# A two-layer hybrid decoder on one Trainium2 core: first stage with scaled evacuations on VectorE, layout copies partly on GpSimd, projections ahead of matrices, and an output projection that sums attention first

## The chip, the core and the metric

The kernel runs on one core of one Trainium2 chip. The core has a matrix engine (TensorE, PE in the profile, with its weight loads shown apart as PEld), VectorE (DVE), ScalarE (ACT), GpSimd (POOL) and a queue that issues most of the transfers (SyncE, SP). The engines run side by side, each through its own queue in order, and wait for each other on semaphores. SBUF is the working memory with 128 partitions; PSUM holds the results of matmuls in banks of 512 float32 columns.

The metric is the device time of one execution in microseconds. Three executions of the kernel before took 1601.77, 1602.78 and 1603.46 us, so the median is 1602.78 us.

## The reference, cut to what is computed

Batch 1, 256 tokens, width 1024, two layers. The change touches layer 0's mixing stage and, by a shared function, the output projections.

```python
h = rmsnorm(x, norm_mix[0]); memn = rmsnorm(mem, norm_mem[0])
p = h @ w_in_a[0]                        # 1024 columns: 768 for S5, 256 for the queries
mix = s5_mixer(p[..., :768], ...)        # 48 groups x 16 channels, 64 complex states each
ca = memory_cross_attn(p[..., 768:], memn, w_kv_mem[0])      # 4 heads of 64
x = x + concat([mix, ca], -1) @ w_out[0]
x = x + swiglu(rmsnorm(x, norm_ffn[0]), ffn_w_gate[0], ffn_w_up[0], ffn_w_down[0])
# layer 1: RWKV-7 mixing | cross-attention with norm_mem[1], w_kv_mem[1]; then top-2-of-8 experts
return rmsnorm(x, norm_final)

def s5_mixer(u, ...):                    # per group: state x_t = a * x_{t-1} + B_bar u_t  (complex, diagonal a)
    y = Re(C x) + d_skip * u             # B_bar and a are worked out from lam, log_dt, b
    y = gelu(y); return y * sigmoid(y @ w_glu + b_glu)
```

## The kernel before, in words

The program is one long function, `build`, without loops on the device. A planner orders it: it walks the traced instructions with a time model and gives each engine the ready instruction that stands earliest in the program. What stands earlier in the source therefore has priority, but each engine's queue is fixed before the run, and it is worked off in order. A block `with tc.issue_after(ins)` pins what is traced in it behind `ins` on its engine.

Everything that the change touches lies in the first stage (from the pools named `psA`, `wpA`, `acA`, `wkA`, `s5`) and in `outproj`, which opens the second stage. The first stage does, in program order:

- **Normalised input.** `rstd` and a scaled copy give `xh`; `transT` (L193) transposes four 128x128 blocks to one PSUM tile and evacuates them, each times its gain column, into `hT`: blocks 0 and 2 on ACT (L207), blocks 1 and 3 on DVE (L205). Four such calls fill `hT` (8 blocks x 256 tokens).
- **Parameters.** Many small DVE operations on 128x24 tiles turn lambda, dt and B, C into `wre, wim` (for B) and `are, aim` (powers of a).
- **Matrices B.** `blocks` (L488) multiplies `bnat` with `wre, wim` on DVE (two L494 and one L495 a call) and copies the result to `BN` on ACT (two L498 a call). It is called for 12 of the 24 state blocks at a time. Then `cT` and `C0` are copied out of a transposed C on ACT (L515); `cT` takes over the buffer `n1` of `bnat`.
- **Projections.** `project(n)` (L522) multiplies `hT` with 256 columns of `w_in_a` (L529) for n = 0..3: 0 to 2 are the S5 inputs, 3 the queries. It copies the PSUM tile to `U` in a token order by four (L534) and then, with 16 copies of 32 partitions out of PSUM (L538, ACT), to `Um`, the layout that the state matmuls read. The projection's weights are two halves of 512 KB in a ring of four buffers (`wpA`).
- **Local matrices.** With `BN` and `C0`, 384 passes of 32x32 blocks (L577) make `KD_`, which ACT copies out (L581); 48 transposes of `BN` (L585) make `BT`, copied by ACT (L586). `project(2)` is pinned behind the last of these transposes (L589).
- **Memory.** The generator `memory` (L540) normalises and transposes the two halves of `mem`, and evacuates each block twice, times the gains of layer 0 and of layer 1, into `memT[0]` and `memT[1]` (L556, ACT, 32 of them).
- **Rotation.** `Ec, Es` (cosine and sine per time step) are doubled up on DVE (L605 to L610), then `blocks` is called again for `CA` (which is the same memory as `BN`).
- **The loop over q = 0..5.** `front(q)`: 16 passes (L671) from `BT` and `Um`, the rotation (L675 to L678) and two scans (L681) on DVE. `back(q)`: two products on POOL (L688, L689), sums on DVE, matmuls with `KD_` (L695) and `CA` (L701), gelu (L707), the gate matmul (L710), tanh (L711) and the pair `cat0` in high and low part (L713 to L715). Three steps of a `filler` stand between front and back: `keys_values(0)` (L644, 64 passes), `cross` for two token halves, and `keys_values(1)`; what is left of it comes after the loop.
- **Output projection.** `outproj` (L280) loads `w_out` in two tiles of 2 MB; `split` cuts each into four parts of two k-blocks, a high part by a cast on ACT (L183) and a low part by a subtraction on DVE (L184), and `mm3` multiplies three products per k (L189 to L191). The k-blocks 0 to 5 of `cat0` are the S5 part, 6 and 7 the attention. The buffer of the first `w_out` tile (`wpB`) lies on the four buffers of `wpA`, whose last readers are the matmuls of `keys_values(1)`.

Layer 0's feed-forward, the RWKV stage and the experts follow, and are not touched except that layer 1 calls the same `transT` and `outproj`.

Of the kernel before, what the change touches and what calls it, by code (L numbers as in the profile page):

```python
# [9 lines left out]
F32 = mybir.dt.float32  # L10
# [3 lines left out]
OP = mybir.AluOpType  # L14
# [3 lines left out]
P = 128  # L18
# [31 lines left out]
def build(ctx, tc, a, out, taps=None):  # L50
# [57 lines left out]
    def col(nm, i):  # L108
        j = COL[nm] + i
        return cols[:, j:j + 1]  # L110

    def colb(nm, n, w):
        return cols[:, COL[nm]:COL[nm] + n, None].to_broadcast([P, n, w])

    def wload(k, n, *parts, size=2048, cut=1):

        t = ring["w"].tile([P, size], F32, name="w", tag="w")
        v = t[:, :k * n].rearrange("p (k n) -> p k n", n=n)
        for c0, ap in parts:
            src = ap.rearrange("(k p) n -> p k n", p=P)  # L120
            for i in range(0, k, k // cut):
                with ExitStack() as s_:
                    if isinstance(ring["w"], Ring) and "last" in ring:
                        s_.enter_context(tc.issue_after(ring["last"].ins))
                    ring["last"] = dma(v[:, i:i + k // cut, c0:c0 + ap.shape[1]], src[:, i:i + k // cut])
        return v
# [39 lines left out]
        return (pl.tile(shape, F32R, name=name + "h", tag=name + "h", **kw),  # L166
                pl.tile(shape, F32R, name=name + "l", tag=name + "l", **kw))

    def split(pl, w, parts, size=4096, eng=None, last=None):

        k, n = w.shape[1], w.shape[2]
        kp = k // parts if k % parts == 0 else -(-k // parts)
        for k0 in range(0, k, kp):
            kn = min(kp, k - k0)
            src = w[:, k0:k0 + kn, :]
            hi, lo = mkpair(pl, [P, size // parts], "ws")
            hv, lv = (t[:, :kn * n].rearrange("p (k n) -> p k n", n=n) for t in (hi, lo))
            if last and k0:
                with tc.issue_after(last[0]), tc.issue_after(last[1]):
                    S.copy(hv, src)  # L180
                    G.tensor_sub(lv, src, hv.bitcast(F32))
            else:
                S.copy(hv, src)  # L183
                (eng or V).tensor_sub(lv, src, hv.bitcast(F32))  # L184
            yield hv, lv, k0
# [7 lines left out]
    def transT(src, h, q, tr, gain, f32=None, pair=None, act=False):  # L193

        hs = slice(h * P, (h + 1) * P)
        t = tr()
        for j in range(4):
            k = 4 * q + j
            r = TE.transpose(t[:, j, :], src[:, k * P:(k + 1) * P], ident).ins
        for j in range(4):  # L200
            k = 4 * q + j
            g = col(gain[0], gain[1] + k)
            if f32 is not None:
                if j % 2 and not act:
                    V.tensor_scalar(f32[:, k, hs], t[:, j, :], g, None, op0=OP.mult)  # L205
                else:
                    S.activation(f32[:, k, hs], t[:, j, :], AF.Copy, scale=g)  # L207
            if pair:
                S.activation(pair[0][:, k, hs], t[:, j, :], AF.Copy, scale=g)
                V.scalar_tensor_tensor(pair[1][:, k, hs], t[:, j, :], g, pair[0][:, k, hs].bitcast(F32),  # L210
                                       op0=OP.mult, op1=OP.subtract)
        return r
# [67 lines left out]
    def outproj(i, cp, ws, mm, order):  # L280


        for n in range(2):
            ns = slice(n * 512, (n + 1) * 512)
            w = wload(KD, 512, (0, a["w_out"][i][:, ns]), size=4096)
            ps = [mm() for _ in range(NH)]

            def part(h, wh, wl, k0):
                hs = slice(h * P, (h + 1) * P)
                for j in range(2):  # L290
                    k = k0 + j
                    mm3(ps[h], (cp[0][:, k, hs], cp[1][:, k, hs]), wh[:, j, :], wl[:, j, :], k == 0, k == KD - 1)
            ps_ = []
            for p_ in split(ws, w, 4):
                part(0, *p_)
                ps_.append(p_)
            resid(0, n, ps[0])
            yield 0, n
            for j_, p_ in enumerate(ps_):
                with ExitStack() as s_:  # L300
                    if n and j_ > 1 and j_ - 4 >= -len(order):
                        s_.enter_context(tc.issue_after(order[j_ - 4]))
                    part(1, *p_)
            resid(1, n, ps[1])
            yield 1, n


    with ExitStack() as st:
# [188 lines left out]
                s = slice(64 * g, 64 * g + 64)  # L497
                S.copy(v[s, :, :, g, :], m1[s])  # L498

        b0, b1 = bnat[:, 0], bnat[:, 1]  # L500
        for i0 in (0, 12):
            blocks(BN, 0, (b0, b1), wre, wim, OP.subtract, i0, 12)
            blocks(BN, 1, (b1, b0), wre, wim, OP.add, i0, 12)
        cT = su.tile([P, 2, NST, 16], F32, name="cT", tag="n1")
        for ri, sg in ((0, 1.0), (1, -1.0)):
            t = tr()
            for b in range(3):
                TE.transpose(t[:, b, :], cnat[:, ri, 2 * b:2 * b + 2].rearrange("c q p -> c (q p)"), ident)
            tv = t[:, 0:3, :].rearrange("s b (i g j) -> s b i g j", i=4, g=2)
            for d, js in ((cT[:, ri], None), (C0[:, :, ri], True)):  # L510
                dv = d.rearrange("s (b r i) j -> s b r i j", b=3, r=2)
                for r in range(2):
                    for g in range(2):
                        o = dv[64 * g:64 * g + 64, :, r]
                        S.activation(o[:, :, :, 16 * g:16 * g + 16] if js else o, tv[64 * r:64 * r + 64, :, :, g, :],  # L515
                                     AF.Copy, scale=sg)

        U = sp.tile([P, QC, 4, NC], F32, name="U")
        Um = sp.tile([P, NST, NC], F32, name="Um")
# [2 lines left out]
        def project(n):  # L522
            w = w0 if n == 0 else halves(a["w_in_a"][0][:, n * T:(n + 1) * T])
            ps = mm().rearrange("p (c t) -> p c t", c=2)
            for t_ in ((slice(0, P), slice(P, T)) if n == 0 else (slice(0, T),)):
                for c in range(2):
                    cs = slice(c * P, (c + 1) * P)
                    for k in range(KD):
                        TE.matmul(ps[:, c, t_], w[k // 4][:, k % 4, cs], hT[:, k, t_], start=k + c + t_.start == 0,  # L529
                                  stop=k == KD - 1, skip_group_check=True)  # L530
            if n == 3:
                S.copy(qT, ps)
                return
            S.copy(U[:, 2 * n:2 * n + 2], ps.rearrange("p c (t s) -> p c s t", s=4))  # L534
            for w_ in range(4):
                for m in range(4):
                    src = ps[32 * w_:32 * w_ + 32].rearrange("p c (t s) -> p c t s", s=4)[:, :, :, 3 - m]
                    S.copy(Um[32 * m:32 * m + 32, 8 * n + w_:8 * n + 8:4], src)  # L538

        def memory():  # L540

            for h in range(NH):
                m = wk.tile([P, D], F32, name="mrow", tag="xh", bufs=2)
                dma(m, mem[h * P:(h + 1) * P, :])
                xh = wk.tile([P, D], F32, name="xh", tag="xh", bufs=2)
                rs = rstd(m, xh)
                S.activation(xh, m, AF.Copy, scale=rs)
                for q in range(2):
                    t = tr()
                    for j in range(4):  # L550
                        k = 4 * q + j
                        TE.transpose(t[:, j, :], xh[:, k * P:(k + 1) * P], ident)
                    for i in range(2):
                        for j in range(4):
                            k = 4 * q + j
                            S.activation(memT[i][:, k, h * P:(h + 1) * P], t[:, j, :], AF.Copy,  # L556
                                         scale=col("nmem", i * KD + k))
                yield

        memT = [ac.tile([P, KD, T], F32, name="memT", tag=f"memT{i}", bufs=1) for i in range(2)]  # L560
        mem_ = memory()
        project(0)
        project(1)

        id32 = su.tile([P, 32], F32, name="id32")
        V.tensor_reduce(id32, ident.rearrange("p (w c) -> p c w", w=4), axis=AX.X, op=OP.add)
# [2 lines left out]
        for q0, n in ((0, 4), (4, 2)):  # L569
# [9 lines left out]
            for w_ in range(4):  # L579
                o = slice(32 * w_, 32 * w_ + 32)  # L580
                S.copy(KD_[o, q0:q0 + n, :, o], tv[o, :n])  # L581
        for i in range(0, NST, 2):
            t = tr()
            for j in range(4):
                bt_ = TE.transpose(t[:, j, :], BN[:, i + j // 2, j % 2, :], ident).ins  # L585
            S.copy(BT[:, i:i + 2].rearrange("p i r s -> p (i r s)"), t.rearrange("p j s -> p (j s)"))  # L586

        next(mem_)
        with tc.issue_after(bt_):  # L589
            project(2)  # L590
        next(mem_)
        project(3)

# [18 lines left out]
                cn, sn = double(4 * n, cn, sn)  # L612
            n *= 2

        for i0 in (0, 12):
            blocks(CA, 0, (cT[:, 0], cT[:, 1]), are, aim, OP.add, i0, 12)
            blocks(CA, 1, (cT[:, 1], cT[:, 0]), are, aim, OP.subtract, i0, 12)

        with tc.issue_after(early[0]):
            G.memset(gmask, 1.0)  # L620
# [1172 lines left out]
```

## Time and profile before

| what | us |
|---|---|
| median of three executions | 1602.78 |
| the profiled execution's own time | 1604.18 |
| its span, first to last instruction | 1602.4 |
| S5 part of the first stage ends (last `cat0` pair) | 151.5 |
| first matmul of the output projection | 155.8 |

The page of the profile shows all engines over the span: PE busy 95%, DVE 80%, ACT 68%, POOL 9%. These shares belong to the experts above all, which take the larger part of the span. The first stage, about a tenth of the span, has to be read by itself: with the view of stretches, which gives each engine's busy time between two moments, and with the timeline, which lists the instructions in order of time (start, duration, engine, line, operation, output and inputs, count, and in brackets the idle time before with what ended it).

### The profile page before, as it was taken

The page shows a single profiled execution, that of the slowest core. Times are in us where ns is not written, and L with a number is a line of the kernel's source. Part 1 is how long each engine was busy: PE and PEld are TensorE (multiplying, and loading weights), DVE is VectorE, ACT ScalarE, POOL GpSimd, SP SyncE. Part 2 cuts the span into 40 slices and gives each one's busy share as a digit, 9 for nine tenths or more (in the row PEclk, how much of TensorE's full clock was granted, in tenths as well). Part 3 has the DMA queues.
Part 4 walks back from the last instruction along what each step waited for, and adds up shares of the span by engine and source line. Part 5 has one row for each costly group of instructions (what it writes and reads, how often), then busy time and mean ns, then how long its engine had stood idle before and what let it go on. Part 6 is the DMA issues. An engine that isn't in the chain of part 4 may idle for free. (4 is left out here: it accounts for less than half of the span.)

```text
span 1602.4 us, 21869 instructions
## 1 busy us (share of the span) xinstructions
PE 1515.7 (95%) x8465; PEld 1272.6 (79%) x8465; DVE 1276.7 (80%) x1567; ACT 1087.6 (68%) x1417; POOL 139.9 (9%) x183
## 2 busy tenths in 40 slices
PE   5798999998969889999999999999999999999996
PEld 4686888887968768888888888888888888888885
DVE  7744655545796568899899899899899898988986
ACT  6765554435634337777787787787777778777774
POOL 2033000003564130000000000000000000000000
PEclk9799999999989989999999999999999999999999
DMA  6023654622310677999999999999999999999970
GB/s 181 15 93 127 238 199 143 217 99 89 122 50 21 224 285 275 347 374 356 342 379 354 345 374 360 343 370 366 339 369 367 363 349 362 350 356 365 355 278 29
DMA packets 198031, 423.46 MB, mean 264 GB/s; under 512 B 13952, under 2 KB 35614, under 8 KB 197918
## 3 DMA queue, kind: packets, MB, share of 16 engines
q1 hardware_dynamic: 195746, 419.29, 71.5%
q10 hardware_dynamic: 2172, 2.68, 0.5%
q8 instruction: 68, 1.11, 0.3%
q14 instruction: 45, 0.37, 0.1%
HBM read 420.91 MB, written 1.05 MB: 263 GB/s over the span
## 5 line engine op out<-in xcount | busy, mean ns | idle before, releaser
L184 DVE TENSOR_TENSOR wsl<-w,wsh 128x1024 fp32r<-128x1024 f32 (+1 forms) x757 | 894.2, 1216 | 149.9 <-ACT wsh L183 138.1
L183 ACT CAST wsh<-w 128x1024 fp32r<-128x1024 f32 (+1 forms) x757 | 783.4, 1049 | 248.9 <-PE gu L191 95.6
L190 PE MATMUL gu<-wsl,xeh 128*128 128x512 f32 x896 | 350.0, 391 | 0.0
L189 PE MATMUL gu<-wsh,xeh 128*128 128x512 f32 x896 | 348.1, 395 | 1.6 <-DVE xs L1697 1.6
L191 PE MATMUL gu<-wsh,xel 128*128 128x512 f32 x896 | 348.9, 389 | 0.0
L189 PEld LDWEIGHTS gu<-wsh,xeh 128*128 128x128 f32 x896 | 168.3, 188 | 37.3 <-ACT wsh L183 2.4
L191 PEld LDWEIGHTS gu<-wsh,xel 128*128 128x128 f32 x896 | 168.2, 188 | 35.3 <-DVE xel L1472 0.4
L190 PEld LDWEIGHTS gu<-wsl,xeh 128*128 128x128 f32 x896 | 168.2, 188 | 34.8
L190 PE MATMUL yac<-wsl,ath 128*128 128x512 f32 x440 | 173.0, 393 | 0.0
L191 PE MATMUL yac<-wsh,atl 128*128 128x512 f32 x440 | 171.7, 390 | 0.0
L189 PE MATMUL yac<-wsh,ath 128*128 128x512 f32 x440 | 136.3, 391 | 0.0
L277 POOL TENSOR_TENSOR rs<-vv,mhalf 128x1 f32<-128x1 f32 x8 | 4.4, 557 | 1204.8 <-DVE vv L276 1204.8
L191 PEld LDWEIGHTS yac<-wsh,atl 128*128 128x128 f32 x440 | 82.7, 188 | 17.1
L189 PEld LDWEIGHTS yac<-wsh,ath 128*128 128x128 f32 x440 | 82.2, 188 | 16.9
L190 PEld LDWEIGHTS yac<-wsl,ath 128*128 128x128 f32 x440 | 82.8, 188 | 15.4
L190 PE MATMUL mm<-wsl,hTh 128*128 128x512 f32 (+1 forms) x192 | 71.3, 371 | 0.0
L189 PE MATMUL mm<-wsh,hTh 128*128 128x512 f32 (+1 forms) x192 | 71.1, 374 | 0.0
L191 PE MATMUL mm<-wsh,hTl 128*128 128x512 f32 (+1 forms) x192 | 70.3, 372 | 0.0
L1659 ACT CAST ath<-t 128x512 fp32r<-128x512 f32 x55 | 32.3, 587 | 30.9 <-PE yac L190 30.2
L1651 DVE TENSOR_TENSOR sg<-sg,gu 128x512 f32<-128x512 f32 x56 | 38.2, 682 | 13.7 <-PE gu L191 13.7
L191 PE MATMUL dn<-hTh,wsC 128*128 128x256 f32 x160 | 46.5, 291 | 1.0 <-POOL wsC L1149 0.9
L189 PE MATMUL dn<-hTh,wsC 128*128 128x256 f32 x160 | 46.1, 288 | 0.0
(533 smaller groups left out, 2052.8 us busy)
## 6 DMA issues: line engine op xcount, KB each, us to landing
w<-in_moe_w_gate_dram SPq DMA_DIRECT2D x55, 2048.0 KB
w<-in_moe_w_up_dram SPq DMA_DIRECT2D x55, 2048.0 KB
w<-in_moe_w_down_dram SPq DMA_DIRECT2D x54, 2048.0 KB
w<-in_w_in_b_dram SPq DMA_DIRECT2D x22, 512.0 KB
w<-in_ffn_w_gate_dram SPq DMA_DIRECT2D x5, 2048.0 KB
w<-in_ffn_w_up_dram SPq DMA_DIRECT2D x5, 2048.0 KB
w<-in_ffn_w_down_dram SPq DMA_DIRECT2D x5, 2048.0 KB
w<-in_w_out_dram SPq DMA_DIRECT2D x4, 2048.0 KB
```

The costliest lines, as they stand in the source:

```text
L183: S.copy(hv, src)
L184: (eng or V).tensor_sub(lv, src, hv.bitcast(F32))
L189: TE.matmul(ps, xp[0], wh, start=start, stop=False, skip_group_check=True)
L190: TE.matmul(ps, xp[0], wl, start=False, stop=False, skip_group_check=True)
L191: TE.matmul(ps, xp[1], wh, start=False, stop=stop, skip_group_check=True)
L277: hold.append(G.tensor_tensor(rs, vv, mhalf, op=OP.pow).ins)
L1651: V.tensor_mul(sg, sg, ps[1])
L1659: S.copy(at[0], t)
```

## The change: what it does

- `transT` with a float32 target evacuates its four blocks by one VectorE multiplication with a broadcast tile of gains (new function `gains`) instead of four scaled copies on ACT and DVE. `memory` does the same for `memT[0]` and `memT[1]`.
- `blocks` runs over three groups of 8 state blocks instead of two of 12, for `BN` and for `CA`. The copies to `cT` and `C0` stand ahead of it, and `cT` has a buffer of its own (`n3`).
- The 16 small copies to `Um` read `U` in SBUF instead of PSUM; for n = 0 they stay on ACT, for n = 1 and 2 they go to GpSimd.
- `project(0)`, `(1)` and `(2)` stand one after the other; the transposes to `BT` follow them, ahead of the local matrices, and the pin on `project(2)` is gone.
- `outproj` for layer 0 takes the k-blocks in the order 6, 7, 0 to 5 (`split` gets a starting point `turn`); layer 1 keeps its order.

```diff
+    def gains(nm, i):
+        return cols[:, COL[nm] + i:COL[nm] + i + 4, None].to_broadcast([P, 4, P])
...
-    def split(pl, w, parts, size=4096, eng=None, last=None):
+    def split(pl, w, parts, size=4096, eng=None, last=None, turn=0):
...
-        for k0 in range(0, k, kp):
+        for k0 in [*range(turn, k, kp), *range(0, turn, kp)]:
...
+        if f32 is not None:
+            V.tensor_mul(f32[:, 4 * q:4 * q + 4, hs], t, gains(gain[0], gain[1] + 4 * q))
         for j in range(4):
             k = 4 * q + j
             g = col(gain[0], gain[1] + k)
-            if f32 is not None:
-                if j % 2 and not act:
-                    V.tensor_scalar(f32[:, k, hs], t[:, j, :], g, None, op0=OP.mult)
-                else:
-                    S.activation(f32[:, k, hs], t[:, j, :], AF.Copy, scale=g)
...
-                    mm3(ps[h], (cp[0][:, k, hs], cp[1][:, k, hs]), wh[:, j, :], wl[:, j, :], k == 0, k == KD - 1)
+                    mm3(ps[h], (cp[0][:, k, hs], cp[1][:, k, hs]), wh[:, j, :], wl[:, j, :], k == k_0,
+                        k == (k_0 - 1) % KD)
+            k_0 = 0 if i else QC
             ps_ = []
-            for p_ in split(ws, w, 4):
+            for p_ in split(ws, w, 4, turn=k_0):
...
-        b0, b1 = bnat[:, 0], bnat[:, 1]
-        for i0 in (0, 12):
-            blocks(BN, 0, (b0, b1), wre, wim, OP.subtract, i0, 12)
-            blocks(BN, 1, (b1, b0), wre, wim, OP.add, i0, 12)
-        cT = su.tile([P, 2, NST, 16], F32, name="cT", tag="n1")
+        cT = su.tile([P, 2, NST, 16], F32, name="cT", tag="n3")
         for ri, sg in ((0, 1.0), (1, -1.0)):
...
+        b0, b1 = bnat[:, 0], bnat[:, 1]
+        for i0 in range(0, NST, 8):
+            blocks(BN, 0, (b0, b1), wre, wim, OP.subtract, i0, 8)
+            blocks(BN, 1, (b1, b0), wre, wim, OP.add, i0, 8)
...
-                    src = ps[32 * w_:32 * w_ + 32].rearrange("p c (t s) -> p c t s", s=4)[:, :, :, 3 - m]
-                    S.copy(Um[32 * m:32 * m + 32, 8 * n + w_:8 * n + 8:4], src)
+                    (S.copy if n == 0 else G.tensor_copy)(Um[32 * m:32 * m + 32, 8 * n + w_:8 * n + 8:4],
+                                                         U[32 * w_:32 * w_ + 32, 2 * n:2 * n + 2, 3 - m, :])
...
-                        for j in range(4):
-                            k = 4 * q + j
-                            S.activation(memT[i][:, k, h * P:(h + 1) * P], t[:, j, :], AF.Copy,
-                                         scale=col("nmem", i * KD + k))
+                        V.tensor_mul(memT[i][:, 4 * q:4 * q + 4, h * P:(h + 1) * P], t,
+                                     gains("nmem", i * KD + 4 * q))
...
-        project(0)
-        project(1)
+        for n in range(3):
+            project(n)
+        for i in range(0, NST, 2):
+            t = tr()
+            for j in range(4):
+                TE.transpose(t[:, j, :], BN[:, i + j // 2, j % 2, :], ident)
+            S.copy(BT[:, i:i + 2].rearrange("p i r s -> p (i r s)"), t.rearrange("p j s -> p (j s)"))
...
-        for i in range(0, NST, 2):
-            t = tr()
-            for j in range(4):
-                bt_ = TE.transpose(t[:, j, :], BN[:, i + j // 2, j % 2, :], ident).ins
-            S.copy(BT[:, i:i + 2].rearrange("p i r s -> p (i r s)"), t.rearrange("p j s -> p (j s)"))
...
-        with tc.issue_after(bt_):
-            project(2)
...
-        for i0 in (0, 12):
-            blocks(CA, 0, (cT[:, 0], cT[:, 1]), are, aim, OP.add, i0, 12)
-            blocks(CA, 1, (cT[:, 1], cT[:, 0]), are, aim, OP.subtract, i0, 12)
+        for i0 in range(0, NST, 8):
+            blocks(CA, 0, (cT[:, 0], cT[:, 1]), are, aim, OP.add, i0, 8)
+            blocks(CA, 1, (cT[:, 1], cT[:, 0]), are, aim, OP.subtract, i0, 8)
```

## The prediction, written before the changed kernel was run

> **What bounds the kernel now.** The change lies in the first stage, so the view of stretches comes first, cut where TensorE's state changes (busy us and count of each engine, then the granted clock, DMA share, GB/s):
>
> ```profile
> 10.90:29.80 18.90, 18.60 (x121) 17.23 (x121) 17.01 (x106) 11.11 (x31) 3.21 (x9) 1.00 0.75 193
> 29.80:69.40 39.60, 19.52 (x476) 17.25 (x475) 32.53 (x73) 29.54 (x64) 1.23 (x1) 0.73 0.10 33
> 69.40:149.50 80.10, 76.67 (x767) 64.83 (x766) 35.11 (x73) 48.94 (x118) 26.80 (x26) 0.98 0.19 63
> 149.50:155.80 6.30, 0.26 (x2) 0.14 (x2) 1.96 (x10) 1.99 (x4) 2.43 (x9) 0.87 1.04 400
> ```
>
> The columns are PE, PEld, DVE, ACT, POOL. PE is full from 10.9 to 29.8 and again, but for 80.10 - 76.67 = 3.4 us, from 69.4 to 149.5. Between them is a hole: 39.60 - 19.52 = 20.1 us without a matmul, with DMA at a tenth of its share. The last stretch is a second gap of 6.0 us in which only DMA is full. What opens the hole is told by PE's waits from 29.8 to 69.4 (total us, times, longest):
>
> ```profile
> PE bu L577 <- ACT C L515: 10.8, 3, 10.3
> PE trp L585 <- ACT BT L586: 4.7, 2, 3.0
> PE bu L577 <- ACT BC L498: 2.6, 2, 2.0
> ```
>
> All three are ACT's copies for the matrices. PE stands behind them in its queue while `project(2)`, pinned behind the last `BT` transpose, would have work. What ends the stage is in the timeline:
>
> ```profile
> 142.72 3.19 PE L644 MATMUL mm<-w,memT 128*128 128x256 f32 x14
> 145.93 4.27 SPq L63 DMA_DIRECT2D w<-in_w_out_dram  x2
> 148.87 0.70 PE L710 MATMUL yp<-yg,glu 128*128 128x256 f32 x2 [0.22 <-ACT yg L707]
> 151.02 0.45 DVE L715 SCALAR_TENSOR_TENSOR catl<-yq,cath 128x256 fp32r<-128x256 f32 x1 [0.48 <-ACT cath L714]
> 154.70 3.89 ACT L183 CAST wsh<-w 128x1024 fp32r<-128x1024 f32 x4 [3.71 <-DMA w<-in_w_out_dram]
> 155.80 1.22 PE L189 MATMUL mm<-wsh,cath 128*128 128x512 f32 x2 [6.04 <-ACT wsh L183]
> ```
>
> The last `keys_values(1)` matmul ends at 142.72 + 3.19 = 145.91; 0.02 us later `w_out` is issued into the memory that it frees; the tile lands at 154.7 and PE starts at 155.8, which is 9.9 us after that matmul and 4.3 us after the S5 part is ready (151.47). So the stage is TensorE's work plus its 20.1 us hole, then one load behind the last memory matmul.
>
> **The change part by part.** First the projections:
>
> ```profile
> 24.97 5.23 SPq L63 DMA_DIRECT2D w<-in_w_in_a_dram  x4
> 69.64 5.77 PE L529 MATMUL mm<-hT,w 128*128 128x256 f32 x20
> 75.69 1.46 PE L529 MATMUL mm<-hT,w 128*128 128x256 f32 x6
> 77.42 8.37 PE L529 MATMUL mm<-hT,w 128*128 128x256 f32 x38
> ```
>
> The 64 passes are `project(2)` and `(3)`: 5.77 + 1.46 + 8.37 = 15.6 us, 7.8 each. With the pin gone, `project(2)` can run from 29.8, since its weights are issued at 24.97, when `project(0)` frees its buffers, and DMA has room. It fills 7.8 us of the hole. `project(3)` needs the buffers of `project(1)`, free at 29.8, and stands next in the program; it covers 7.8 us more wherever the copies of the matrices still hold PE. Behind them the memory transposes and `keys_values(0)` are available earlier too, since the ring of weights moves up with the projections in SP's queue: the `w_kv_mem` halves, now issued from 76.75, follow as soon as `project(2)` is done. In PE's queue `project(2)` stands before the `BT` transposes: if its weights came late, these and the local matrices would wait with it.
>
> Now the elementwise work, by line with shapes apart (busy us, mean ns):
>
> ```profile
> L207 ACT ACTIVATE hT<-trp,cols 128x128 f32<-128x128 f32 x8 | 2.8, 364 | 4.0 <-DVE hT L205 2.2 <-PE trp L199 1.7
> L205 DVE TENSOR_SCALAR hT<-trp,cols 128x128 f32<-128x128 f32 x8 | 2.8, 345 | 0.0
> L556 ACT ACTIVATE memT<-trp,cols 128x128 f32<-128x128 f32 x32 | 8.5, 422 | 1.7 <-PE trp L552 1.7
> L538 ACT COPY Um<-mm 32x128 f32<-32x128 f32 x48 | 12.3, 257 | 0.5
> L498 ACT COPY BC<-m 64x768 f32<-64x768 f32 x16 | 13.3, 830 | 4.8 <-DVE m L495 4.4
> L650 ACT COPY kT<-mm 64x512 f32<-64x512 f32 x4 | 2.3, 580 | 2.2 <-PE mm L644 2.2
> L714 ACT ACTIVATE cath<-yq 128x256 fp32r<-128x256 f32 x6 | 2.5, 416 | 2.1 <-DVE yq L713 2.0
> L494 DVE TENSOR_TENSOR m<-bnat,wre 128x768 f32<-128x768 f32 x4 | 3.7, 951 | 0.0
> L605 DVE TENSOR_TENSOR tb<-Es,c 128x384 f32<-128x384 f32 x3 | 1.6, 549 | 0.0
> L675 DVE TENSOR_TENSOR Y<-bu,Ec 128x512 f32<-128x512 f32 x6 | 4.1, 679 | 12.5 <-PE bu L671 12.5
> ```
>
> *ACT* loses 2.8 for `hT`, 8.5 for `memT` and two thirds of 12.3 for `Um`, 8.2. The blocks become 24 copies of 64x512 instead of 16 of 64x768: by the row of that shape 24 x 0.58 = 13.9 against 13.3. Together -18.9 us. The 16 copies that stay read SBUF; an operation of twice the columns takes 0.42 us there (L714), so they lie below that, at 0.26 as now if the source makes no difference, and cost at most 16 x 0.16 = 2.6 us more, beside PE. ACT had 39.60 - 29.54 = 10.1 us idle in the hole, and gets rid of the 4.3 us blocks of `Um` copies that stood between the matrices, so it costs PE no more than the turn of the two PSUM tiles of transposes: the 4.7 us of waits on `BT` above, of which I keep 3.
>
> *DVE* gains operations that multiply 512 columns of PSUM, as L675 does: 4 x 0.68 = 2.7 for `hT` in place of 2.8, and 8 x 0.68 = 5.4 for `memT`. A 512-column product of the blocks lies between 549 (384) and 951 (768), in proportion 0.683; 36 of them are 24.6 us against 24 x 0.951 = 22.8. Together +7.1 us. Between 29.8 and 69.4 DVE was idle for 39.60 - 32.53 = 7.1 us, most of it behind `cT`, which is now copied ahead of the blocks. The two cancel, so the first rotated product still starts about when it does now:
>
> ```profile
> 67.57 0.68 DVE L675 TENSOR_TENSOR Y<-bu,Ec 128x512 f32<-128x512 f32 x1
> 93.53 0.64 ACT L707 ACTIVATE yg<-yp 128x256 f32<-128x256 f32 x1
> 102.84 1.09 PE L701 MATMUL yp<-U,BC 128*32 128x63 f32 x64
> L681 DVE TENSOR_TENSOR_SCAN Y<-R,Y 128x256 f32<-128x256 f32 x12 | 8.1, 713 | 4.2 <-ACT R L679 4.1
> L688 POOL TENSOR_TENSOR U<-Y,Es 128x512 f32<-128x512 f32 x6 | 7.7, 1278 | 14.6 <-issue 7.7 <-DVE Y L681 4.6 <-DVE nm L236 2.3
> ```
>
> From there to the first gelu takes 26 us now, because PE had the projections and the memory in between; by its own operations about 8: two products of 0.68 and two sums of 0.41 (a row below has one), two scans of 0.71, two POOL products of 1.28, two more sums, and 1.09 for the matmuls with `CA`. From the first gelu to the last pair the loop takes 151.47 - 93.53 = 57.9 us. So the S5 part would be ready at 67.6 + 8 + 57.9 = 133.5, 18 us earlier. If the cover on DVE fails, each us that DVE is late makes this end a us later.
>
> *POOL* takes 32 copies of 32x128, an operation that the trace doesn't show. Rows of its lines and two places where DVE runs beside it:
>
> ```profile
> L620 POOL MEMSET gmask<- 128x128 f32 x1 | 0.2, 206 | 0.0
> L623 POOL TENSOR_SCALAR_AFFINE_SELECT gmask<-gmask 128x128 f32<-128x128 f32 x1 | 0.4, 356 | 0.1
> L247 POOL TENSOR_SCALAR pr<-pr,rc 128x256 f32<-128x256 f32 x8 | 8.1, 1018 | 9.8 <-DVE rc L242 9.8
> 76.90 1.47 POOL L689 TENSOR_TENSOR U<-Y,Ec 128x512 f32<-128x512 f32 x1
> 77.15 1.49 DVE L678 TENSOR_TENSOR Y<-Y,T 128x256 f32<-128x256 f32 x1
> 122.23 2.30 POOL L247 TENSOR_SCALAR pr<-pr,rc 128x256 f32<-128x256 f32 x2
> 123.40 0.41 DVE L678 TENSOR_TENSOR Y<-Y,T 128x256 f32<-128x256 f32 x1
> ```
>
> A copy costs between 0.21 and 1.02 us; I take 0.36, the row that reads as many columns from one input. 32 of them are 11.5 us (6.6 to 32.6), on an engine busy 1.2 us in the hole, and `Um` for n = 1 is first needed by the third round. Queued behind them are the root for the second half of `mem` (L160), for which ACT, the transposes and `keys_values(0)` wait, and the gate masks. The copies run beside DVE's block products and rotation, all of them with two inputs in SBUF. A DVE sum took 1.49 instead of 0.41 us beside POOL's two-input product, and 0.41 beside its one-input scaling. By the second row the copies cost DVE nothing; by the first each may cost up to its own length, 11.5 us for all at 0.36. I take the second, as a copy has one input, and keep both ends.
>
> The Trainium skill (SBUF — State Buffer, section "Who interferes with whom") says that a DVE instruction with two SBUF inputs and a GpSimd instruction that reads SBUF exclude each other for the whole instruction. The 1.49 agrees, the 0.41 inside two scalings doesn't show it; by the page the sum would lose up to those 11.5 us on DVE.
>
> *The output projection* multiplies the same 24 products a tile half in another order. Attention first helps only if the weights are there before the S5 part; with the load as the last to come it is worth 0, else at most the six passes on k = 6, 7 (6 x 0.61 = 3.7 us by the row at 155.80).
>
> **Sum.** PE's hole of 20.1 less 3 left: 17. At the end `keys_values(1)` has the lowest priority and ended 149.57 - 145.91 = 3.7 us before PE's last S5 pass; with S5 freed first it may end last, and then all 3.7 us come back in front of the 9.9 us load. I take half, 2. So 15 us: 1604.18 - 15 = 1589.2 for the profiled execution, which was 1.4 above the median: **1588**. What follows is full of PE work and moves up unchanged.
>
> **The rivals.**
> - *POOL holds DVE, and S5 sets the end.* If each copy costs half of L247's 1.02 us for half its columns, and holds DVE for that long, 32 x 0.51 = 16.3 us: Y starts at 84 and the S5 part is ready at 149.8. The weights land before; the six attention passes are done by then, so the second stage stands as if it had started at 149.8 - 3.7 = 146.1 instead of 155.8: 1593. For: the 1.49 row. Against: the 0.41 row. The page's rule leads here too. Chance 0.18.
> - *Only `project(2)` moves.* PE still waits for the matrices, and `keys_values(1)` ends last: 7.8 - 3.7 = 4, 1598. For: all three waits are on ACT copies that stay. Against: `project(3)` needs nothing from them. Chance 0.12.
> - *Slower: the same lock at its dear end.* At 1.02 us a copy, 32.6 us on DVE: Y at 100, the S5 part ready at 166.1, the second stage as if started at 162.4, 6.6 us late: 1609. It decides from 155.8 + 3.7 - 133.5 = 26 us, 0.81 us a copy. For: POOL's scaling of twice the columns does take 1.02. Against: it didn't hold DVE. Chance 0.07.
> - *It doesn't do what it says:* the planner puts `project(2)` behind the matrices again, since it orders by its own times: 1603, chance 0.07.
>
> **How the numbers follow.** The forecast has 0.56, with 1582 (hole wholly closed and both ends together) to 1594. With the second and third cases faster by over 0.2% (3.2 us, about what a measurement of this kernel can tell from no change) has 0.56 + 0.18 + 0.11 = 0.85, within 0.2% 0.08, slower 0.07. The range reaches from 1579, a hole closed with the 3.4 us behind it, to 1600, and leaves out the last two rivals.
>
> **What would show it.** PE busy without a gap of over 3 us between 30 and 69; L529 with 256 columns ending before 60; POOL's copies under 0.5 us and DVE's 128x512 products at 0.68 beside them; first Y between 65 and 70; the first `w_out` cast near 139. It is wrong if Y comes after 84, if PE waits on `memT`, or if `keys_values(1)` ends later than 136.

## The result and the profile after

| | before | after |
|---|---|---|
| median | 1602.35 us (1601.77 to 1603.46) | 1590.82 us (1590.0 to 1592.38) |
| profiled execution | 1604.18 us, span 1602.4 | 1590.0 us, span 1588.0 |
| first matmul of `keys_values(0)` | 88.91 | 71.82 |
| last matmul of `keys_values(1)` ends | 145.91 | 132.91 |
| first matmul of the output projection | 155.80 | 141.78 |

The ratio after to before is 0.9928, 95% interval 0.9911 to 0.9946: faster by about 11.5 us. In some executions of several of these kernels the whole program ran at a lower granted clock and took some 7 to 28 us longer; the medians and the ratios of the experiments contain them (in `e12_order_um` eight of twelve, while its other four took 1591.60 to 1593.59 us and thirteen of the seventeen of before beside it 1600.87 to 1604.61), so small differences are read from the places in the profiles first.

From the first output-projection matmul to the end of the span takes 1602.4 - 155.8 = 1446.6 us before and 1588.0 - 141.78 = 1446.2 after. The whole gain is that this matmul starts 14.0 us earlier, so the first 156 us are all that has to be read. (The two profiled executions differ by 14.2 us, the medians by 11.5: the one of before lies 1.8 us above its median, the one of after 0.8 below.) The view of stretches of the kernel after, cut where it was cut before (PE, PEld, DVE, ACT, POOL with their counts, granted clock, DMA share, GB/s):

```profile
29.80:69.40 39.60, 34.74 (x558) 29.88 (x557) 34.88 (x77) 27.97 (x52) 18.26 (x34) 0.96 0.27 81
69.40:133.00 63.60, 58.14 (x613) 48.13 (x611) 38.46 (x79) 32.78 (x63) 27.56 (x25) 0.97 0.11 34
```

The hole of 20.1 us is now 39.60 - 34.74 = 4.9. PE's waits in the kernel after from 29.8 to 141.8 (total us, times, longest) show what is left:

```profile
PE trp L568 <- ACT BT L569: 4.4, 1, 4.4
PE mm L193 <- ACT wsh L187: 3.8, 1, 3.8
PE yp L709 <- ACT yg L706: 2.1, 3, 0.9
PE mm L643 <- DVE memT L557: 2.1, 1, 2.1
```

The two waits of 10.3 and 2.6 us on `C` and `BC` are gone. One gap of 4.4 us stays, on the `BT` copies. The timeline of the kernel after at the points that the prediction named:

```profile
42.30 0.59 ACT L537 COPY U<-mm 128x512 f32<-128x512 f32 x1
42.78 1.08 ACT L569 COPY BT<-trp 128x512 f32<-128x512 f32 x2
43.42 0.66 PE L568 MATMUL trp<-ident,BC 128*128 128x128 f32 x4 [4.44 <-ACT BT L569]
59.65 3.83 PE L532 MATMUL mm<-hT,w 128*128 128x256 f32 x17
73.49 0.68 DVE L674 TENSOR_TENSOR Y<-bu,Ec 128x512 f32<-128x512 f32 x1
128.76 4.15 PE L643 MATMUL mm<-w,memT 128*128 128x256 f32 x18
132.94 1.04 SPq L63 DMA_DIRECT2D w<-in_w_out_dram  x2
139.41 0.45 DVE L714 SCALAR_TENSOR_TENSOR catl<-yq,cath 128x256 fp32r<-128x256 f32 x1 [0.48 <-ACT cath L713]
140.68 3.88 ACT L187 CAST wsh<-w 128x1024 fp32r<-128x1024 f32 x4 [1.31 <-DMA w<-in_w_out_dram]
141.78 1.22 PE L193 MATMUL mm<-wsh,cath 128*128 128x512 f32 x2 [3.82 <-ACT wsh L187]
```

`project(3)` is done at 63.5. `w_out` is issued when `keys_values(1)` ends, as before, and now lands 0.8 us after the S5 part is ready (139.86): the two arrive almost together.

### The profile page after: what moved, and what is told of

It is laid out like the page before. It is cut to its first block, busy times and chain, and to the rows that moved or that the text cites. A ratio compares the mean times of both kernels' runs of the same rounds, so it can differ in the third digit from the quotient of the medians.

```text
span 1588.0 us, 21853 instructions
## 1 busy us (share of the span) xinstructions
PE 1516.3 (95%) x8465; PEld 1272.1 (80%) x8465; DVE 1283.0 (81%) x1583; ACT 1073.0 (68%) x1355; POOL 157.7 (10%) x215
## 5 line engine op out<-in xcount | busy, mean ns | idle before, releaser
L1650 DVE TENSOR_TENSOR sg<-sg,gu 128x512 f32<-128x512 f32 x56 | 38.1, 681 | 13.7 <-PE gu L195 13.7
```

What stands on the lines that cost most here:

```text
L1650: V.tensor_mul(sg, sg, ps[1])
```

## The experiments

Every kernel computes the same outputs; only order, engine and the place of buffers change. The measure that tells most is how long PE takes from 29.8 to the first output-projection matmul, split into busy and idle. It is the same work each time (1237 to 1249 matmul records). The stretch 29.80 to that matmul in four kernels, here of before:

```profile
29.80:155.80 126.00, 96.45 (x1242) 82.22 (x1241) 69.59 (x154) 80.47 (x185) 30.46 (x36) 0.90 0.21 71
```

of after:

```profile
29.80:141.78 111.98, 96.52 (x1245) 80.60 (x1243) 76.14 (x168) 64.69 (x121) 48.57 (x69) 0.96 0.23 74
```

of the new order alone (`e1_reorder`):

```profile
29.80:156.41 126.61, 106.54 (x1249) 87.90 (x1247) 68.26 (x153) 83.20 (x190) 31.67 (x36) 0.86 0.20 65
```

and of the order with the layout copies (`e12_order_um`):

```profile
29.80:146.19 116.39, 99.00 (x1247) 83.99 (x1245) 71.78 (x153) 73.39 (x157) 44.34 (x69) 0.92 0.21 72
```

| kernel | KV(0) starts | output projection starts | PE busy + idle from 29.8 | ratio, 95% interval |
|---|---|---|---|---|
| before | 88.91 | 155.80 | 96.45 + 29.55 | |
| e1: order alone | 87.27 | 156.41 | 106.54 + 20.07 | 0.9981 [0.9954, 1.0009] |
| e9: `Um` copies alone | 84.67 | 152.63 | 97.21 + 25.62 | 0.9977 [0.9944, 1.0011] |
| e10: `memT` on DVE alone | 89.71 | 158.17 | 99.36 + 29.01 | 0.9991 [0.9959, 1.0024] |
| e11: `hT`, `memT`, `Um` | 87.18 | 154.91 | 102.11 + 23.00 | 0.9971 [0.9941, 1.0001] |
| e12: order and `Um` | 80.13 | 146.19 | 99.00 + 17.39 | 0.9971 [0.9919, 1.0023] |
| e2: after, old order and pin | 77.77 | 142.53 | 96.54 + 16.19 | 0.9915 [0.9886, 0.9945] |
| e4: after, `Um` on ACT | 82.37 | 150.63 | 97.78 + 23.05 | 0.9987 [0.9956, 1.0019] |
| e5: after, `memT` on ACT | 72.78 | 146.34 | 99.47 + 17.07 | 0.9939 [0.9910, 0.9969] |
| e6: after, old blocks | 71.90 | 144.10 | 97.06 + 17.24 | 0.9918 [0.9890, 0.9946] |
| e3: after, k from 0 | 72.24 | 142.05 | 96.92 + 15.33 | 0.9909 [0.9874, 0.9944] |
| after | 71.82 | 141.78 | 96.52 + 15.46 | 0.9928 [0.9911, 0.9946] |

(KV(0) is `keys_values(0)`; each ratio is to the kernel before, run beside it.)

### e1: the new order alone

```diff
-        project(0)
-        project(1)
+        for n in range(3):
+            project(n)
+        (the BT transposes here)
...
-        with tc.issue_after(bt_):
-            project(2)
```

> The kernel before with one part of the change: project(0), (1), (2) in a row, the BT transposes right behind them, no pin. All evacuations, Um copies, blocks and the order of the output projection as before. Theory (TensorE's hole is refilled because project(2) no longer waits behind the matrices): most of the 14 us come from here, 7 to 12 us off, 1591 to 1596, and the hole between 29.8 and 69.4 falls from 20 us to under 12. Rival (the gain is the load taken off ScalarE, the order alone does little): 0 to 3 us off, 1600 to 1603.

Measured: 1602.99 us, no gain, which is the rival's time; yet the hole is filled, as the theory said. Its stretches:

```profile
29.80:69.40 39.60, 33.89 (x527) 27.93 (x526) 27.61 (x65) 33.18 (x83) 0.00 (x0) 0.83 0.26 83
76.00:92.00 16.00, 11.26 (x42) 9.77 (x41) 10.07 (x18) 11.48 (x38) 6.53 (x5) 0.50 0.00 1
```

Idle in the first stretch is 5.7 us instead of 20.1. But over the whole way to the output projection idle fell by 9.5 us (29.55 to 20.07) while the same matmuls took 10.1 us longer (96.45 to 106.54). The second row says why: from 76 to 92 PE had only half its clock. By line, 4.7 of the 10.1 us are the passes of `keys_values` (35.0 against 30.3 us) and 1.4 those on `BT` and `Um` (13.7 against 12.3). The timeline of this kernel there:

```profile
74.30 0.66 PE L552 MATMUL trp<-ident,xh 128*128 128x128 f32 x4 [1.66 <-ACT BT L568]
75.96 4.23 ACT L556 ACTIVATE memT<-trp,cols 128x128 f32<-128x128 f32 x16
82.61 1.15 ACT L547 ACTIVATE xh<-mrow,rs 128x1024 f32<-128x1024 f32 x1 [1.10 <-POOL rs L160]
83.82 1.97 PE L552 MATMUL trp<-ident,xh 128*128 128x128 f32 x8 [3.26 <-ACT xh L547]
86.85 4.22 ACT L556 ACTIVATE memT<-trp,cols 128x128 f32<-128x128 f32 x16
87.27 1.22 PE L641 MATMUL mm<-memT,w 128*128 128x256 f32 x2 [1.48 <-ACT memT L556]
88.28 4.47 PE L641 MATMUL mm<-w,memT 128*128 128x256 f32 x10
94.03 4.58 PE L641 MATMUL mm<-memT,w 128*128 128x256 f32 x20
```

With its projections done, PE runs out of work behind `memT`, which ACT makes at 76.0 and 86.9, hardly sooner than before (75.9 and 88.0). The granted clock is at 0.50 by then, and the long passes pay: ten take 4.47 us where twenty take 4.58 once the clock is back. By the clock records of the trace the half clock began at 76.07, and the stretches around it read:

```profile
72.65:76.07 3.42, 1.77 (x16) 1.77 (x17) 3.35 (x9) 3.32 (x6) 0.44 (x1) 1.00 0.00 0
76.07:93.13 17.06, 12.32 (x44) 10.56 (x44) 11.14 (x19) 11.79 (x39) 6.86 (x6) 0.50 0.00 1
```

So one wait of 1.66 us was enough here, and the half clock outlasted the next two, of 3.26 and 1.48 us. The Trainium skill (TensorE: Matmul & The Clock Gate, section "Part 1: The HAM clock gate") says that an idle window of about 3.4 us drops the array to half rate until it has been busy about as long. The rows agree only in part: the half rate lasted five times 3.41 us, but in the 3.42 us ahead of it PE was idle for 1.65 us, not for all of them.

### e9, e10, e11: the reliefs of ACT alone

`e9_um_alone` takes the `Um` lines of the change into the kernel before, `e10_mem_alone` the `memT` lines, `e11_relief` the `hT`, `memT` and `Um` lines with the old order and blocks:

```diff
-                    S.copy(Um[32 * m:32 * m + 32, 8 * n + w_:8 * n + 8:4], src)
+                    (S.copy if n == 0 else G.tensor_copy)(Um[32 * m:32 * m + 32, 8 * n + w_:8 * n + 8:4],
+                                                         U[32 * w_:32 * w_ + 32, 2 * n:2 * n + 2, 3 - m, :])
...
-                            S.activation(memT[i][:, k, h * P:(h + 1) * P], t[:, j, :], AF.Copy,
-                                         scale=col("nmem", i * KD + k))
+                        V.tensor_mul(memT[i][:, 4 * q:4 * q + 4, h * P:(h + 1) * P], t,
+                                     gains("nmem", i * KD + 4 * q))
```

> The kernel before with one part alone: the Um copies read U, those of n = 1 and 2 on GpSimd. Theory now (ScalarE's copies, in a row from 24 to 92 us, set when the first keys_values(0) matmul can start, 88.9 before; the rest of the stage takes 65 to 70 us from there): 8 us off ScalarE are worth 5 to 8 us, 1594 to 1597, and the first L644 comes near 82. Rival (the relief only pays together with the new order): 0 to 2 us off.

> The kernel before with one part alone: memT multiplied out by VectorE, 8 products instead of 32 scaled copies on ScalarE. Theory now: the second half of memT is on the path itself (75.9 to 92.2), so 4 to 8 us off, 1594 to 1598, first L644 near 82. Rival (VectorE's products wait behind the rotation and the blocks in its queue, or delay them): 0 to 2 us off.

> The kernel before with all three reliefs of ScalarE (hT, memT, Um), in the old order, with the old blocks and the old output projection. Theory now: nearly all of the gain, 1590 to 1594. Rival (early cT and the smaller blocks carry a part, as they let the matrices start): 1595 to 1599.

Measured: 1601.73, 1607.21 and 1600.55 us, beside a median of 1603.47 for before; none differs from before by its interval. All three theories miss, and the rival of `e11_relief` too. `e10_mem_alone` looks slower rather than equal: eleven of its twelve executions took 1606.06 to 1609.71 us, 29 of the 35 of before 1601.32 to 1605.72. A theory that ACT's relief is the whole gain falls with `e11_relief`. (Its profiled execution, 1604.20, is among its five longest; the other seven took 1598.08 to 1601.12, so the places in its profile may be later than in most.) In its timeline the pinned projection still waits for the last `BT` transposes, whose copies ACT makes between other copies:

```profile
63.02 3.76 PE L584 MATMUL trp<-ident,BC 128*128 128x128 f32 x16 [1.66 <-ACT BT L585]
66.58 5.49 PE L530 MATMUL mm<-hT,w 128*128 128x256 f32 x20
85.79 1.04 PE L553 MATMUL trp<-ident,xh 128*128 128x128 f32 x8
```

`project(2)` starts at 66.58, at a slow clock as in the kernel before (20 passes in 5.49 us; 5.77 there), and the second half of the memory is transposed behind it at 85.79, so KV(0) starts at 87.18.

### e12: the order with the layout copies

The edits of `e1_reorder` and `e9_um_alone` together, nothing else.

> The kernel before with two parts alone: projections 0 to 2 in a row ahead of the BT transposes with no pin, and the Um copies read from U with 32 of 48 on GpSimd. hT, memT, the blocks and the output projection are as before. Either part alone gave nothing (1602.99 and 1601.73). Theory of the pair (a free TensorE queue and a relieved ScalarE are both needed, and Um is the larger part of the relief): first keys_values(0) matmul between 76 and 81, first output-projection matmul between 144 and 149, 1592 to 1597, ratio 0.993 to 0.997. Rival, that the other ScalarE reliefs (memT and hT on VectorE) are needed as well: first keys_values(0) matmul at 83 or later, output projection at 152 or later, 1600 to 1603, ratio 0.998 to 1.000.

Measured: KV(0) at 80.13 and the output projection at 146.19, both within the theory's bounds and far from the rival's; the profiled execution is 1593.04. The ratio, 0.9971 with an interval that holds 1, can't confirm that; the four executions named with the result (1591.60 to 1593.59 us) and the places in the profile can. Each edit alone moved the output projection by +0.6 and -3.2 us, both by -9.6. The timelines show the link. In `e1_reorder`, ACT:

```profile
47.47 0.59 ACT L534 COPY U<-mm 128x512 f32<-128x512 f32 x1
47.95 4.27 ACT L538 COPY Um<-mm 32x128 f32<-32x128 f32 x16
52.25 1.07 ACT L568 COPY BT<-trp 128x512 f32<-128x512 f32 x2
```

In `e12_order_um`, ACT and PE:

```profile
44.24 0.59 ACT L534 COPY U<-mm 128x512 f32<-128x512 f32 x1
44.73 1.08 ACT L568 COPY BT<-trp 128x512 f32<-128x512 f32 x2
75.06 1.97 PE L552 MATMUL trp<-ident,xh 128*128 128x128 f32 x8 [6.24 <-ACT xh L547]
```

The projection moved ahead brings its own block of 4.27 us of `Um` copies into ACT's queue, ahead of the `BT` copies; on POOL that block is out of the way. What this kernel still lacks against the kernel after is in the last line: 6.24 us of PE waiting for the second half of the memory.

### e2, e4, e5, e6, e3: one part of the change undone

`e2_pin_back` puts the old order and the pin back into the kernel after, `e4_um_act` the `Um` copies on ACT, `e5_mem_act` the `memT` scaling on ACT, `e6_blocks_back` the blocks by 12 with `cT` behind them, and `e3_order07` the old order of the products:

```diff
-                    (S.copy if n == 0 else G.tensor_copy)(Um[32 * m:32 * m + 32, 8 * n + w_:8 * n + 8:4],
+                    S.copy(Um[32 * m:32 * m + 32, 8 * n + w_:8 * n + 8:4],
...
-            k_0 = 0 if i else QC
+            k_0 = 0
```

> The changed kernel with the old order back: project(0), (1), local matrices, BT transposes, project(2) pinned behind them. Theory: it loses 7 to 12 us against the changed kernel, 1598 to 1603. Rival (relief of ScalarE): it keeps most of the gain, 1591 to 1595, as the copies that held the matrices are gone all the same.

> The changed kernel with all 48 Um copies on ScalarE, reading U. If GpSimd's 32 copies (0.51 us each) hold VectorE through the shared port, the rotation's 128x384 products go back from 0.64 to 0.55 us, and the first Y comes 2 to 4 us earlier; but ScalarE gets 32 x 0.30 = 9.6 us between the matrices. I expect the second to weigh more: 1 to 5 us slower, 1592 to 1596. Rival (the port is the dearer): 1 to 3 us faster, 1588 to 1590.

> The changed kernel with memT evacuated by ScalarE again, 32 scaled copies. Theory now (two things must both be early before keys_values(0) can start: TensorE's projections, which need the new order or early matrices, and the memory's second half, which needs ScalarE to be free): 3 to 6 us slower than the changed kernel, 1594 to 1597, first L643 near 78 instead of 71.8. Rival (VectorE's products delay the blocks as much as they relieve ScalarE, as in the run with memT alone): within 1.5 us, 1590 to 1592.

> The changed kernel with the blocks by 12 again and cT behind them in the buffer of bnat. Theory now: as ScalarE has room, this costs little, 1590 to 1594. Rival (the early cT is what lets the matrices be ready): 3 to 6 us slower, 1594 to 1597.

> The changed kernel with the output projection in its old order, k-blocks 0 to 7. In the changed kernel w_out comes 0.8 us after the S5 part is ready, so the order should be worth nothing: 1590 to 1592. Rival (attention first is part of the gain): 2 to 4 us slower, 1593 to 1595.

Measured: 1592.61, 1598.96, 1594.47, 1593.21 and 1591.87 us. Four of the five keep most of the gain; only without the `Um` part on GpSimd is most of it lost (0.9987). For `e2_pin_back` that is the rival; `e3_order07` and `e6_blocks_back` came as expected. `e4_um_act` lost more than its theory said, and its first Y came at 74.73, later than in the kernel after (73.49) and not 2 to 4 us earlier. Its `Um` copies read `U` in SBUF too, so what counts is their engine and not their source. `e5_mem_act` has the time forecast for it, but not the way: KV(0) starts at 72.78, not near 78, and the loss comes behind it, 2.95 us of it in busy time. The pin is no obstacle once the matrices come early: in `e2_pin_back` the pinned projection starts when the last `BT` is done, and that is at 53.6, not at 66.6 as in `e11_relief`. The two differ in the smaller blocks with the early `cT` and in the order of the products, and the latter is worth nothing (`e3_order07`); the blocks and `cT` alone were not run.

```profile
53.30 0.59 ACT L588 COPY BT<-trp 128x512 f32<-128x512 f32 x1 [0.25 <-PE trp L587]
53.59 4.48 PE L532 MATMUL mm<-hT,w 128*128 128x256 f32 x20
```

With `Um` on ACT, the gap on `BT` grows from 4.4 to 6.5 us, and KV(0) starts 10.6 us later. In `e4_um_act`:

```profile
44.14 1.11 PE L568 MATMUL trp<-ident,BC 128*128 128x128 f32 x4 [6.53 <-ACT BT L569]
```

The order of the products is worth nothing that can be measured (output projection at 142.05 against 141.78).

### e7, e8: the weights of the output projection earlier

If the load behind `keys_values(1)` is the last to come, the first `w_out` tile in memory that is free earlier should let S5 set the start. `e7_wout_early` swaps the two buffers of the ring for the last loads, and issues the gains ahead of the loop; `e8_wout_early07` does so with products from k = 0.

```diff
-        ring["w"] = pool(st, "wpB", 2)
+        wpB = [pool(st, "wpB0", 1), pool(st, "wpB1", 1)]
+        ring["w"] = Ring(wpB, (1, 0))
```

> A version that may beat both: the changed kernel, with the first w_out tile in the second buffer of the ring, over memory of hT, qT and memT[0] (free once the last scores are done, near 106) instead of over the weight ring of keys_values(1) (free at 132.9), and the last column vectors loaded ahead of the loop, since their row tile lies there too. If the load behind the last memory matmul is what the stage still waits for (3.8 us of PE waiting at 141.78), the first product starts near 134.5, as soon as the split tiles are free, and the S5 part (139.9) comes last: 3 to 6 us faster than the changed kernel, 1585 to 1588. Rival (the split tiles or the banks come free no earlier, or the early load collides): 0 to 1 us.

> The same with the output projection in its old order, 0 to 7. With the weights early, attention first has 18 products of the first half that need nothing of the last two S5 quarters, the old order 12; at 0.63 us each both cover the 5 us until the S5 part is ready, so I expect the same time as with attention first, within 1 us. Rival (now the order matters): 2 to 4 us slower than that run.

Measured: 1591.99 us (0.9938 [0.9901, 0.9974]) and 1589.36 (0.9931 [0.9899, 0.9963]), which can't be told from the kernel after. The theory's 134.5 for the first product was missed: in the profile of `e7_wout_early` the output projection starts at 138.97, 2.8 us earlier than in the kernel after, and in that of `e8_wout_early07` at 139.41:

```profile
105.18 26.73 SPq L63 DMA_DIRECT2D w<-in_w_out_dram  x2
137.57 0.42 ACT L713 ACTIVATE cath<-yq 128x256 fp32r<-128x256 f32 x1 [0.49 <-DVE yq L712]
137.89 5.76 ACT L187 CAST wsh<-w 128x1024 fp32r<-128x1024 f32 x6
138.97 1.22 PE L193 MATMUL mm<-wsh,cath 128*128 128x512 f32 x2 [2.41 <-ACT wsh L187]
```

The weights are issued at 105, and now the casts stand behind the last `cath` in ACT's queue: S5 is the end. Here too attention first gained nothing.

## Why the prediction was right, and where not

The time forecast was 1588 in 1579 to 1600 and came out at 1590.8. That it came so near is in part luck: the hole was filled and the stage ended as forecast, but three errors in the terms were offset or covered. The terms, one by one.

**PE's hole.** Forecast 20.1 to 3, measured 20.1 to 4.9, so 15.2 of the forecast 17 us. Behind it idle grew: up to the end of `keys_values(1)` PE was idle 5.5 us from 69.4 on, against 3.2 before. The load behind it took 8.9 us instead of 9.9. 15.2 - 2.3 + 1.0 = 13.9, within rounding the 14.0 by which the output projection moved. The forecast's 17 - 2 = 15 was a us too much. The 2 us have the right size for another reason than the one given: in front of `keys_values(0)` PE waits 2.1 us for `memT`, which the prediction had named as a sign of being wrong, and the sixteen passes behind that wait take 5.18 us, against 3.72 in `e7_wout_early`, where it is 0.35.

**What failed is the cause given for it:** that `project(2)` fills the hole "with the pin gone", and that a us of hole is a us of time. `e1_reorder` takes the pin away and fills the hole, and gains nothing; `e2_pin_back` puts the pin back and loses nothing that can be told. What the runs show in its place is a condition of two parts: the projections must stand where PE can reach them (by order, or by matrices that are done early), and ACT must be free enough that what follows comes early too. With one of the two, idle shrinks (by 9.5 us in `e1_reorder`, 6.6 in `e11_relief`), but stalls remain ahead of long passes, which then run at half the clock: busy time grows by 10.1 and 5.7 us. The forecast charged a stall its length and not the slow passes behind it. In the kernel before the hole was followed by the small matmuls of the matrices, to which the clock matters less. Those of before, at clock 0.50, and of after, at 1.00:

```profile
49.34 2.02 PE L577 MATMUL bu<-C,BC 128*32 128x32 f32 x128 [0.24 <-issue]
54.47 1.03 PE L583 MATMUL bu<-C,BC 128*32 128x32 f32 x96
```

That is 1.5 times as long for each, where the long passes double, and for all 384 about 2 us. Moving work moved the stalls to where the clock matters.

**ACT, -18.9 us.** The size was about right: ACT's busy time from 29.8 to the output projection fell from 80.47 to 64.69, 15.8 us, with a part of the relief ahead of 29.8. But the text used it only to say that ACT costs PE no more than 3 us. The `Um` copies are the part that decides: `e4_um_act` against after is 8.8 us of the 14.0, and `e12_order_um`, with `Um` as its only relief, has 9.6.

**DVE, and the first Y at 67.6.** It came at 73.49, 5.9 us late: the two terms of 7.1 did not cancel. From 29.8 to Y, DVE's busy time grew by 7.9 us (30.70 to 38.59), of which `memT` is 5.0 and the stretching by POOL's copies, below, 2.9; but of its 7.1 us of idle only 2.0 were used up. The waits on `cT` (4.5 us) went, and waits of 4.9 us on ACT's copies of the smaller blocks came. In the kernel after:

```profile
32.89 0.69 DVE L497 TENSOR_TENSOR m<-bnat,wre 128x512 f32<-128x512 f32 x1 [2.54 <-ACT BC L501]
37.56 1.46 DVE L497 TENSOR_TENSOR m<-bnat,wre 128x512 f32<-128x512 f32 x2
```

From Y to the S5 part the forecast had 8 + 57.9 = 65.9 us and the trace has 139.86 - 73.49 = 66.4. That is luck: the first gelu came 15.5 us behind Y (89.03) and not 8, and the loop from there took 50.8 us and not 57.9. So S5 was ready at 139.9 instead of 133.5. It cost nothing, since the weights landed only at 140.7; in `e7_wout_early` it is the limit.

**POOL, 0.36 us a copy.** Measured 0.47 in the mean, 15.0 us for 32. The rival with 0.51 a copy had the price of POOL nearly right, but not what it does to DVE. The kernel after, during the copies (34.8 to 51.1) and behind them:

```profile
34.81 16.32 POOL L540 COPY Um<-U 32x128 f32<-32x128 f32 x32 [11.76 <-ACT U L537]
36.44 1.35 POOL L540 COPY Um<-U 32x128 f32<-32x128 f32 x2
47.53 0.64 DVE L604 TENSOR_TENSOR tb<-Es,c 128x384 f32<-128x384 f32 x1
47.79 1.64 POOL L540 COPY Um<-U 32x128 f32<-32x128 f32 x3
51.46 0.55 DVE L609 TENSOR_TENSOR Es<-Es,tb 128x384 f32<-128x384 f32 x1
```

And `e9_um_alone`, where DVE stands still from 79.7 to 87.0:

```profile
79.85 4.56 POOL L537 COPY Um<-U 32x128 f32<-32x128 f32 x14
```

A copy takes 0.29 us where DVE does nothing (22 copies of that kernel, 0.28 to 0.29 each). Beside DVE it takes DVE's pace: 0.65 us beside products of 0.77, 0.52 beside 0.64, 0.32 beside 0.44. DVE in turn loses little: 32 of its operations, as many as there are copies, are 0.08 to 0.10 us longer than the same ones in `e4_um_act` (0.64 instead of 0.55), 2.9 us in all and not the length of a copy each. The Trainium skill (SBUF — State Buffer, section "Who interferes with whom") says that a DVE instruction with two SBUF inputs and a GpSimd instruction that reads SBUF contend, and that the order of issue decides which of them blocks. These rows agree with that, and it is mostly the copy that waits; the prediction had read the rule as DVE standing still for each copy. Both rivals on POOL fall.

**The smaller terms.** Attention first at 0, right (`e3_order07`, `e8_wout_early07`). `keys_values(1)` ended at 132.9; the sum has it between 145.91 - 17 = 128.9 and 3.7 later, 132.6. The first cast came at 140.7 for "near 139". It did not end last on PE: 5.0 us before the last S5 pass (3.7 before), so the 2 us taken off for that were not lost there. `project(3)` moved too (done at 63.5, 85.8 before), so the rival with `project(2)` alone falls. Of the signs, four failed: a PE gap of 4.4 us (over 3), `project(3)` at 63.5 (after 60), DVE's products at 0.73 to 0.77 beside the copies (0.68), Y at 73.5 (after 70). Of the three signs of being wrong one came, the wait on `memT`. None of them took the time out of its range.

**Open** is how the differences among `e2`, `e3`, `e6` and after, all within some 3 us, divide among the parts, whether the 2.8 us of `e7_wout_early` last in a median, and why `memT` on DVE alone (`e10_mem_alone`) moved the output projection 2.4 us later. Its trace shows only how: PE is at half clock once more, from 122.97 to 126.38, and busy time grows by 2.9 us while idle shrinks by 0.5. Open too is whether the smaller blocks and the early `cT` would do anything alone.

## What to carry to other kernels

Price an idle hole by what happens when it is filled: follow the next instruction that needs another engine (here `memT` and the `BT` copies on ACT), and if the stall only moves in front of long matmuls, add the passes that run at half the clock to its length. Where two parts of a change each remove one of two conditions, neither shows anything alone; undo parts from the changed kernel and add pairs to the old one before calling a part worthless. Split a stretch into busy and idle for the same work: a busy time that grows points to the clock, and the granted clock where it grows tells.

## What was not expected of the hardware

- The granted clock made as much of the difference as idle time: the same 1240 or so matmuls took 96.45 us of PE before and 106.54 in `e1_reorder`. The mean clock of the stretch doesn't tell it alone (0.90 and 0.86, but 0.96 with 96.52 us after): it matters which passes run at half.
- It took less than 3.4 us of idle to lose the clock: 1.65 in 3.42 us in `e1_reorder`.
- POOL's one-input copies of 32x128 took 0.29 us alone, 0.47 in the mean beside DVE's two-input operations, and slowed these by some 0.09 us each; POOL's two-input products held DVE longer (`Y` at L677: 1.49 us beside one, 0.41 without).
- ACT's copy of 32x128 takes 0.296 us from SBUF and 0.257 from PSUM; the prediction had left open whether the source matters.
